# Attention: raw queries in the scores, the norm factor applied per token to the biased scores

## The chip, the cores and the metric

The kernel runs on one core of a Trainium2 chip. Five engines work side by side: TensorE (PE; its weight loads are listed as PEld), VectorE (DVE), ScalarE (ACT), GpSimd (POOL) and SyncE (SP, which only issues transfers here). The metric is the device time in microseconds; several runs are made, and their median is given.

## The reference

One step of a two-layer decoder over 1024 prompt tokens and 8 sample tokens, width 1024, all in fp32: layer 0 has a recurrent mixer, layer 1 sliding-window attention, and each is followed by a squared-ReLU MLP. The change lies in layer 1's attention: 16 query heads on 4 key/value heads of 64 columns, window 128, a linear distance bias per head, one learned sink per head, and an RMS norm of every query and key head.

```python
def rms_norm(x, g):
    xf = x.astype(jnp.float32)
    y = xf * lax.rsqrt(jnp.mean(xf * xf, axis=-1, keepdims=True) + RMS_EPS)
    return (y * g.astype(jnp.float32)).astype(x.dtype)

def qkv_heads(x, w_qkv, q_g, k_g):
    n, t, _ = x.shape
    q, k, v = jnp.split(x @ w_qkv, [Q_DIM, Q_DIM + KV_DIM], axis=-1)
    q = rms_norm(q.reshape(n, t, N_KV, GROUP, HEAD_DIM), q_g)
    k = rms_norm(k.reshape(n, t, N_KV, HEAD_DIM), k_g)
    return q, k, v.reshape(n, t, N_KV, HEAD_DIM)

def sink_attention(q, k, v, dist, mask, sinks):
    s = jnp.einsum('...qkgd,...skd->...kgqs', q, k).astype(jnp.float32) * (HEAD_DIM ** -0.5)
    s = s - alibi_slopes()[:, :, None, None] * dist.astype(jnp.float32)
    s = jnp.where(mask, s, NEG_INF)
    sink = sinks.astype(jnp.float32).reshape(N_KV, GROUP)[:, :, None, None]
    m = jnp.maximum(jnp.max(s, axis=-1, keepdims=True), sink)
    e = jnp.exp(s - m)
    p = e / (jnp.sum(e, axis=-1, keepdims=True) + jnp.exp(sink - m))
    return jnp.einsum('...kgqs,...skd->...qkgd', p.astype(v.dtype), v)
```

The outputs are the token stream, the new recurrent states, and the new keys (normed) and values.

## The kernel before

Tokens lie in the free dimension: a tile is 128 channels by 1032 tokens (T), worked in three chunks (c) of 344 (CH). To keep fp32 accuracy on fast passes, a value is split into a high part and a rest (hi, lo), and a product is three passes: hi·hi, hi·lo, lo·hi. A few small products are done in full fp32 instead; they show as two records each in the trace.

`attention` (L693) goes like this.

- **Projection.** Eight query tiles (t = 0 to 7, two heads each) and two key tiles (p = 0, 1). The first key and query tile are projected together (`proj_many`, L971), then the values (`v_proj`). The other eight units come from a generator, `filler` (L974): per tile `proj_steps` (L767) issues 24 groups of three matmuls into the three banks "P" (L772), one `yield` after each group.
- **Norm before.** `take_out` (L709) copies a finished bank twice on ScalarE (its square, L711, and itself, L712), after which the bank is free. `qk_norm` (L715) sums the squares over each head's 64 channels by a full fp32 matmul with a block matrix (L718, 344 columns, bank "N"), makes the factor in `rstd_m2` (L288: Ln, Exp, Square on ScalarE, L290 to L292; two VectorE operations, L293 and L295; it returns -2/rms) and multiplies (L720). `parts` splits the result (L730, L731), and SP sends its halves to their partitions (L747, L748; for keys L763). A unit has 24 + 1 + 3 = 28 yields.
- **Blocks.** 64 blocks (`STEPS`, L825), each 128 queries of one tile against up to 256 keys. `stage_a` (L840): four score matmuls (L852) into one of two banks "S"; on VectorE one custom operation per head (L856) that adds the bias from PSUM and SBUF, scales by -1 and finds the extreme against the sink; the exponential with its sum on ScalarE (L859); the reciprocal on VectorE (L861); the normalisation on GpSimd (L863). The bias is made on GpSimd once per tile, at its block 0 (`bias_of`, L834, L837). `stage_b`: four transposes (L872) and a copy (L877). `stage_c`, every fourth block: the products with the values (L893) and the split of the output (L900, L901).
- **Order.** The loop of L1013 runs `stage_a` three blocks ahead (`AHEAD`) and takes 3.9 yields of `filler` per block (`TF`) until block 46 (`J0`), where the rest is run out; from block 49 (`J1`) it takes 2.4 yields per block of the output projection (L1038). Under it a scheduler places each engine's instructions in one fixed order ahead of time; on the chip every engine works through its list in order and waits at semaphores.
- **Samples.** `samples` (L928) does the eight sample tokens during the output projection: 16 matmuls with the cached keys as weights (L933), softmax, 16 with the cached values (L958).

Of the kernel before, what the change touches and what calls it, by code (L numbers as in the profile page):

```python
# [60 lines left out]
def trunk(ctx: ExitStack, tc: tile.TileContext, I, O):  # L61
# [38 lines left out]
    def S(s="s"):  # L100
        return small["pool"].tile([P, CH], F32, tag="S", name=nm(s))
# [21 lines left out]
    def r_(x):  # L123
        return x.bitcast(F32R)
# [163 lines left out]
    def rstd_m2(ps, out=None):  # L288
        r0, q = S("r0"), S("q")
        act.activation(q, ps, AF.Ln, bias=eps)  # L290
        act.activation(r0, q, AF.Exp, scale=-0.5)
        last["rstd"] = act.activation(q, r0, AF.Square).ins  # L292
        dve.scalar_tensor_tensor(q, ps, eps, q, ALU.add, ALU.mult)  # L293
        out = r0 if out is None else out
        dve.scalar_tensor_tensor(out, q, -3.0, r0, ALU.add, ALU.mult)  # L295
        return out
# [396 lines left out]
    def attention(hs):  # L693
# [12 lines left out]
        ks = aux[:, P:P + 2 * NS].rearrange("p (t n) -> p t n", t=2)  # L706
        den = [cp.tile([P, 4], F32, name=f"den{i}") for i in range(4)]

# [6 lines left out]
        def qk_norm(sx, gcol):  # L715
            s, x = sx
            st = B("N")[:, :CH]
            pe.matmul(st, lhsT=blk, rhs=s, start=True, stop=True)  # L718
            r = rstd_m2(st)
            dve.scalar_tensor_tensor(x, x, gcol, r, ALU.mult, ALU.mult)  # L720
            return x
# [28 lines left out]
        def k_evac(p, c, sx):  # L750
            if c == 0:
                kst[p] = [(A("kh"), A("kl")) for _ in range(2)]
            k = qk_norm(sx, kg[:, 0:1])
            if c == 2:
                o = 2 * CH
                kout = S("kout")
                pool.tensor_copy(kout[:, :P], k[:, SEQ - P - o:SEQ - o])
                sp.dma_start(O["k"][p], kout[:, :P])
                pool.tensor_copy(ks[:, p, :], k[:, SEQ - o:T - o])
            for n, x in enumerate(parts(k)):  # L760
# [6 lines left out]
        def proj_steps(tag, w, evac):  # L767
# [59 lines left out]
        osm = aux[:, 2 * P:2 * P + 8 * NS].rearrange("p (t n) -> p t n", t=8)  # L827
# [6 lines left out]
        def bias_of(t):  # L834
            for u, hd in enumerate(heads(t)):
                o = (t % 2) * 512 + u * 256
                pool.tensor_scalar(bias2[:, o:o + 256], distM, -SLOPES[hd], 0.0, ALU.mult, ALU.add)  # L837


        def stage_a(j):  # L840
            t, b = STEPS[j]
            p, i = divmod(t, 4)
            if b == 0:
                bias_of(t)
# [9 lines left out]
            for u in range(2):  # L854
                o = (t % 2) * 512 + u * 256 + 256
                dve.tensor_tensor_reduce(  # L856
                    se[:, u, 256 - n:256], s[:, u * 256:u * 256 + n], bias2[:, o - n:o],
                    scale=-1.0, scalar=nsink[:, hd[u]:hd[u] + 1], op0=ALU.add, op1=ALU.min, accum_out=dn[:, u:u + 1])
# [69 lines left out]
        def samples():  # L928
            st = B("N")
# [6 lines left out]
            sb = S("ssb")  # L936
# [4 lines left out]
            dve.tensor_scalar(z[:, 129:257], z[:, 129:257], V("slope_row"), None, ALU.mult)  # L941
            dve.tensor_copy(z[:, 128:129], nsink_row)
            dd = cp.tile([P, 2], F32, name="dd")
            dve.tensor_tensor_reduce(z[:, 0:P], st2[:, :P], z[:, 129:257], scale=-1.0, scalar=nsink_row[:, 0:1],
# [26 lines left out]
        proj_many([wk, wq], hs, lambda i, c, o: (q_evac if i else k_evac)(0, c, take_out(o)))  # L971
        v_proj()

        def filler():  # L974
            for t in range(1, 8):
                if t == 4:
                    yield from proj_steps(("k", 1), unit("k", 1, 1), lambda *a: k_evac(1, *a))
                yield from proj_steps(("q", t), unit("q", t, 1 if t < 7 else 0), lambda *a, t=t: q_evac(t, *a))
# [401 lines left out]
```

## Time and profile before

| what | us |
|---|---|
| median of three runs (2017.08 to 2018.62) | 2017.08 |
| the profiled execution, in all | 2018.72 |
| its span, first to last instruction | 2016.9 |
| VectorE busy in it | 1411.6 |
| ScalarE busy in it | 1054.7 |
| GpSimd busy in it | 321.9 |

The span is what the profile's times add up to; the execution's own time has a little more around it. PE's busy time counts a matmul until its results are out, so overlapping matmuls make it look full: the pace is read from start to start. A group's row gives line, engine, operation, out<-in by the program's names, shape and count; then busy us, mean ns of one, and the idle time before it with what ended it. A row of waits reads: who, at which line, waited for whom: us in total, times, longest. A row of stretches: from:to, length, then busy us and count for PE, PEld, DVE, ACT, POOL; then the granted clock, the DMA engines' share and GB/s.

### The profile page before, as it was taken

Reading aid. Unit: us, or ns where it says so; the run is one execution under the profiler, and the core shown is the slowest. Engines: PE = TensorE matmul, PEld = TensorE weight load, DVE = VectorE, ACT = ScalarE, POOL = GpSimd, SP = SyncE. Lnnn points to the kernel's source line nnn. Section 1 sums busy time; section 2 is a strip of 40 time slices with the busy share of each in tenths; the row PEclk is TensorE's granted clock in tenths of the full one; section 3 lists DMA queues with packets and bytes.
Section 4 is the critical chain, followed back from the end, with each engine's and each line's share of the span. In section 5 each row is a group of like instructions: output and inputs, shape, how many; then the busy total and the mean of one; then the engine's idle time right before and its main releaser. Section 6 shows DMA issues by size and latency. Waiting matters only on the chain.

```text
span 2016.9 us, 38731 instructions
## 1 busy us (share of the span) xinstructions
PE 1995.5 (99%) x15106; PEld 1951.8 (97%) x15106; DVE 1411.6 (70%) x2665; ACT 1054.7 (52%) x2089; POOL 321.9 (16%) x570
## 2 busy tenths in 40 slices
PE   8999999999999999999999999999999999999999
PEld 8999999999999999999998887999999999999999
DVE  7996638877675876766847767579766667766662
ACT  6476536543434655554547776456443436555550
POOL 2420000000002233221004434000000003322220
PEclk9999999999999999999999999999999999999999
DMA  5111242343436788887333436612443447887783
GB/s 179 53 43 53 80 143 78 127 163 137 153 137 215 206 222 227 230 219 156 116 89 87 120 90 199 213 61 96 161 163 127 163 148 249 217 222 214 197 196 106
DMA packets 117927, 305.02 MB, mean 151 GB/s; under 512 B 17512, under 2 KB 50032, under 8 KB 117744
## 3 DMA queue, kind: packets, MB, share of 16 engines
q1 hardware_dynamic: 61744, 135.55, 22.0%
q0 software_dynamic: 28352, 98.30, 19.0%
q10 hardware_dynamic: 27648, 68.70, 9.3%
q8 instruction: 118, 1.93, 0.4%
q14 instruction: 65, 0.53, 0.1%
HBM read 176.30 MB, written 113.51 MB: 144 GB/s over the span
## 4 chain that ended last, share of the span: by engine, by line
PE 92%; DVE 4%; ACT 2%; issue 1%; DMA 1%; POOL 0%; SPq 0%; ACTq 0%; DVEq 0%
PE bD L530 60%; PE bP L227 12%; PE bS L227 6%; PE bP L772 4%; PE bT L227 3%; PE bS L852 1%; PE bO L893 1%; PE bT L872 1%; PE bN L718 1%; DVE sq L278 1%; PE bS L800 1%; DVE wl L167 0%; DMA raw<-w_in 0%; ACT wh L166 0%; DVE t L1189 0%
## 5 line engine op out<-in xcount | busy, mean ns | idle before, releaser
L530 PE MATMUL bD<-op,op 128*128 128x258 f32 x5376 | 648.0, 283 | 0.0
L530 PEld LDWEIGHTS bD<-op,op 128*128 128x128 f32 x5376 | 647.5, 190 | 0.3
L530 PE MATMUL bD<-tl,op 128*128 128x258 f32 x4704 | 567.7, 283 | 0.0
L530 PEld LDWEIGHTS bD<-tl,op 128*128 128x128 f32 x4704 | 566.7, 190 | 0.8 <-ACT he L637 0.3
L543 POOL DMA_DIRECT2D tl<-hsum x196 | 115.2, 698 | 899.1 <-DMA hsum<-he 405.2
L397 DVE TENSOR_TENSOR op<-ws,op 128x512 fp32r<-128x512 f32 (+2 forms) x288 | 170.3, 597 | 79.8 <-ACT op L396 79.8
L403 DVE TENSOR_TENSOR tl<-tl 128x516 fp32r<-128x516 f32 x196 | 130.8, 693 | 123.0 <-ACT tl L402 123.0
L637 ACT COPY ho<-bD 128x516 f32<-128x516 f32 x144 | 85.0, 590 | 243.8 <-PE bD L530 241.6
L396 ACT CAST op<-ws 128x512 fp32r<-128x512 f32 (+2 forms) x288 | 155.8, 550 | 56.0 <-DVE op L397 27.1
L397 DVE TENSOR_TENSOR op<-raw,op 128x512 fp32r<-128x512 f32 (+2 forms) x216 | 124.2, 595 | 57.7 <-ACT op L396 57.7
L637 ACT COPY he<-bD 128x516 f32<-128x516 f32 x144 | 84.0, 583 | 135.3 <-PE bD L530 127.0
L396 ACT CAST op<-raw 128x512 fp32r<-128x512 f32 (+2 forms) x216 | 114.6, 549 | 34.7 <-PE bD L530 22.5
L402 ACT CAST tl<-tl 128x516 fp32r<-128x516 f32 x196 | 114.8, 627 | 2.9 <-DMA tl<-hsum 2.9
L650 ACT ACTIVATE ho<-ho 128x1032 f32<-128x1032 f32 x32 | 34.2, 1069 | 107.2 <-DVE ho L649 107.2
L167 DVE TENSOR_TENSOR wl<-raw,wh 128x1024 fp32r<-128x1024 f32 (+1 forms) x57 | 66.0, 1164 | 23.5 <-ACT wh L166 13.2
L166 ACT CAST wh<-raw 128x1024 fp32r<-128x1024 f32 (+1 forms) x60 | 58.7, 988 | 38.8 <-DMA raw<-w_in 12.9
L863 POOL TENSOR_SCALAR se<-se,den 128x256 f32<-128x256 f32 (+1 forms) x128 | 65.7, 518 | 77.8 <-DVE den L861 75.8
L856 DVE CUSTOM_DVE_ANT_0 se<-bS,bias,nsink 128x256 f32<-128x256 f32 (+1 forms) x128 | 56.4, 461 | 21.2 <-PE bS L852 17.0
L859 ACT ACTIVATE se<-se,den 128x257 f32<-128x257 f32 (+1 forms) x128 | 63.0, 496 | 14.8 <-DVE den L856 13.1
L656 POOL DMA_DIRECT2D spill<-ho x32 | 28.5, 889 | 242.2 <-DVE ho L645 233.2
L645 DVE TENSOR_TENSOR ho<-bD,ho 128x516 f32<-128x516 f32 x72 | 49.7, 690 | 22.9 <-PE bD L530 22.9
L273 ACT ACTIVATE sq<-y 128x344 f32<-128x344 f32 x48 | 23.6, 492 | 71.4 <-DVE y L363 60.8
(300 smaller groups left out, 3727.3 us busy)
## 6 DMA issues: line engine op xcount, KB each, us to landing
tl<-hsum POOLq DMA_DIRECT2D x196, 258.0 KB, 7.8
raw<-w_up SPq DMA_DIRECT2D x64, 512.0 KB, 3.8
raw<-w_dn SPq DMA_DIRECT2D x64, 384.0 KB, 5.9
spill<-ho POOLq DMA_DIRECT2D x32, 516.0 KB, 6.6
spill<-he POOLq DMA_DIRECT2D x32, 516.0 KB, 7.9
hsum<-ho ACTq DMA_DIRECT2D x28, 516.0 KB, 3.6
hsum<-he ACTq DMA_DIRECT2D x28, 516.0 KB, 2.7
hsum<-ts ACTq DMA_DIRECT2D x28, 516.0 KB, 3.5
```

The source lines that it names most:

```text
L167: eng.tensor_tensor(r_(lo[:, sl]), raw[:, sl], hi[:, sl], ALU.subtract)
L227: pe.matmul(o, lhsT=r_(wt[:, col(k):col(k) + P]), rhs=r_(xt[:, cs(c)]), start=(k == first and a == 0), stop=(k == final and a == 2))
L396: act.copy(r_(t[:, 0:n]), src)
L397: dve.tensor_tensor(r_(t[:, n:2 * n]), src, t[:, 0:n], ALU.subtract)
L402: act.copy(r_(hi), lo)
L403: dve.tensor_tensor(r_(lo), lo, hi, ALU.subtract)
L530: pe.matmul(d[:, 512 * b:512 * b + QT], lhsT=r_(wt[:, j * P:j * P + P]), rhs=r_(xt[:, QT * b:QT * b + QT]), start=first and j == 0 and a = ...
L543: pool.dma_start(t[:, n:2 * n], src)
L637: last["copy"] = act.copy(t, f).ins
L772: pe.matmul(ps[c], lhsT=r_(wt[:, k * P:k * P + P]), rhs=r_(xt[:, cs(c)]), start=(k == 0 and a == 0), stop=(k == M8 - 1 and a == 2))
L859: act.activation(se[:, u, 256 - n:257], se[:, u, 256 - n:257], AF.Exp, scale=-1.0, bias=dn[:, u:u + 1], accum_out=dn[:, 2 + u:3 + u])
L863: pool.tensor_scalar(e, e, dn[:, 2 + u:3 + u], 0.0, ALU.mult, ALU.add)
```

## The change

Queries go raw (split, but not normed) into the scores. The key tile carries the keys' norm factor, both norm weights and a constant; the scores of a query token are then short of that token's own factor f. Since (s + d·slope/f)·f = s·f + d·slope, the bias is divided by f per token (GpSimd, per block, into a buffer that alternates by block), and the custom operation on VectorE multiplies by f instead of -1; f and 1/f are per-partition scalars there, because a block has its tokens on partitions. To have them so, the sums of squares are made with the squares as weights and two columns of the block matrix moving: eight matmuls of two columns per query tile, result 128 tokens by 16.

```diff
-    def rstd_m2(ps, out=None):
-        r0, q = S("r0"), S("q")
+    def rstd_m2(ps, out=None, n=CH):
+        r0, q = S("r0")[:, :n], S("q")[:, :n]
...
-        dve.tensor_scalar(qg, V("qg"), -0.0625, None, ALU.mult)
         dve.tensor_scalar(kg, V("kg"), -0.5, None, ALU.mult)
+        dve.tensor_scalar(qg, V("qg"), kg[:, 0:1], None, ALU.mult)
...
+        fac = aux[:, P + 2 * NS:P + 2 * NS + 16 * NS].rearrange("p (t k b u) -> p t k b u", t=4, k=2, u=2)
...
-        def q_evac(t, c, sx):
+        sqs = {}
+
+        def q_evac(t, c, o):
             p, i = divmod(t, 4)
             if c == 0:
                 qs[t] = (A("q0"), A("q1"))
-            q = qk_norm(sx, qg[:, 0:1])
+                sqs[t] = W("sq")
+            act.activation(sqs[t][:, cs(c)], o, AF.Square)
+            hi, lo = S("hi"), S("lo")
+            act.copy(r_(hi), o)
+            dve.tensor_tensor(r_(lo), o, hi, ALU.subtract)
             if c == 2:
-                o = 2 * CH
                 for u in range(2):
                     h = slice(64 * u, 64 * u + 64)
-                    pool.tensor_copy(qblk[h, :, p, u, i], q[h, SEQ - o:T - o])
-            hi, lo = parts(q)
+                    dve.tensor_copy(qblk[h, :, p, u, i], o[h, SEQ - 2 * CH:CH])
...
+        def q_factors(t):
+            s, st = sqs.pop(t), B("N")[:, :2 * NB]
+            for b in range(NB):
+                pe.matmul(st[:, 2 * b:2 * b + 2], lhsT=s[:, b * P:b * P + P], rhs=con[:, C_BLK:C_BLK + P:64], start=True, stop=True)
+            r = S("r")[:, :2 * NB]
+            rstd_m2(st, r, 2 * NB)
+            f = fac[:, t % 4]
+            dve.tensor_scalar(f[:, 0], r.rearrange("p (b u) -> p b u", u=2), 0.0625, None, ALU.mult)
+            dve.reciprocal(f[:, 1], f[:, 0])
...
-            k = qk_norm(sx, kg[:, 0:1])
+            x, r = k_norm(take_out(o))
             if c == 2:
                 o = 2 * CH
-                kout = S("kout")
-                pool.tensor_copy(kout[:, :P], k[:, SEQ - P - o:SEQ - o])
+                kout = S("kout")[:, :P + NS]
+                dve.scalar_tensor_tensor(kout, x[:, SEQ - P - o:T - o], kg[:, 0:1], r[:, SEQ - P - o:T - o], ALU.mult, ALU.mult)
...
+            dve.scalar_tensor_tensor(x, x, qg[:, 0:1], r, ALU.mult, ALU.mult)
+            for n, x in enumerate(parts(x)):
...
-            sx = [take_out(o) for o in ps]
-            yield
-            for c in range(NCH):
-                evac(c, sx[c])
+            yield from evac(ps)
+            done.add(tag)
+
+        def q_out(t):
+            def f(ps):
+                for c in range(NCH):
+                    q_evac(t, c, ps[c])
                 yield
-            done.add(tag)
+                yield
+                q_factors(t)
+                yield
+            return f
...
             for u in range(2):
-                o = (t % 2) * 512 + u * 256 + 256
+                o = (j % 2) * 512 + u * 256 + 256
+                pool.tensor_scalar(bias2[:, o - n:o], distM[:, 256 - n:256], fac[:, t % 4, 1, b, u:u + 1], SLOPES[hd[u]],
+                                   ALU.mult, ALU.mult)
+            for u in range(2):
+                o = (j % 2) * 512 + u * 256 + 256
                 dve.tensor_tensor_reduce(
                     se[:, u, 256 - n:256], s[:, u * 256:u * 256 + n], bias2[:, o - n:o],
-                    scale=-1.0, scalar=nsink[:, hd[u]:hd[u] + 1], op0=ALU.add, op1=ALU.min, accum_out=dn[:, u:u + 1])
+                    scale=fac[:, t % 4, 0, b, u:u + 1], scalar=nsink[:, hd[u]:hd[u] + 1], op0=ALU.add, op1=ALU.min, accum_out=dn[:, u:u + 1])
...
         def samples():
+            sb = S("ssb")
+            act.activation(sb[:, :P], qrow, AF.Square, scale=4.0)
+            st = B("N")
+            pe.matmul(st[:, 0:1], lhsT=sb[:, :P], rhs=ones[:, 0:1], start=True, stop=True)
+            r = S("r")[:, :1]
+            rstd_m2(st[:, 0:1], r, 1)
+            dve.tensor_scalar(dd[:, 2:3], r, 0.0625, None, ALU.mult)
...
+            dve.tensor_scalar(qrow, qrow, V("qg"), None, ALU.mult)
+            yield
```

A key tile is evacuated the same way (`k_out`: three chunks, a yield after each), so every unit now has 24 + 3 = 27 yields; `AHEAD`, `TF` and the rest of the loop's numbers stay. The sample queries are held raw and get their factor in `samples`, as a row's scalar, in the same way.

The scheduler's order moves with it. On TensorE, right behind the last matmul of query tile 1's projection, before (bP: projection, bS: scores, bN: sums of squares):

```order
L772 MATMUL bP_11959<-hh_10798,wl_11717 128x344
L852 MATMUL bS_12034<-kh_11437,q_11491 128x256
L852 MATMUL bS_12034<-kl_11438,q_11491 128x256
L852 MATMUL bS_12034<-kh_11439,q_11492 128x256
L852 MATMUL bS_12034<-kl_11440,q_11492 128x256
L718 MATMUL bN_12062<-sq_12048,con 128x344
L772 MATMUL bP_12121<-hh_10784,wh_11953 128x344
L772 MATMUL bP_12121<-hl_10785,wh_11953 128x344
```

and now:

```order
L787 MATMUL bP_11943<-hh_10798,wl_11682 128x344
L872 MATMUL bS_12016<-kh_11433,q_11487 128x256
L872 MATMUL bS_12016<-kl_11434,q_11487 128x256
L872 MATMUL bS_12016<-kh_11435,q_11488 128x256
L872 MATMUL bS_12016<-kl_11436,q_11488 128x256
L757 MATMUL bN_12064<-con,sq_12034 128x2 x5
L787 MATMUL bP_12089<-hh_10784,wh_11937 128x344
L787 MATMUL bP_12089<-hl_10785,wh_11937 128x344
L787 MATMUL bP_12089<-hh_10784,wl_11938 128x344
L757 MATMUL bN_12064<-con,sq_12034 128x2 x3
```

Where one sum of squares over 344 tokens stood, and two more some way on, a tile's eight small ones now stand in two bursts (16 bursts for the eight tiles).

On GpSimd, around the tenth to fifteenth block, before (se: a block's scores, den: its reciprocal, bias: the bias, aux: sample queries):

```order
L863 TENSOR_SCALAR se_11384<-se_11384,den_11377 128x256 x2
L847 COPY se_11385<-nsink 128x2
L744 COPY aux<-x_12286 64x8 x2
L863 TENSOR_SCALAR se_11385<-se_11385,den_11378 128x256 x2
L847 COPY se_11384<-nsink 128x2
L863 TENSOR_SCALAR se_11385<-se_11385,den_11379 128x256 x2
```

and now (aux holds the factors):

```order
L876 TENSOR_SCALAR bias_11383<-con,aux 128x256 x2
L887 TENSOR_SCALAR se_11385<-se_11385,den_11378 128x256
L867 COPY se_11385<-nsink 128x2
L887 TENSOR_SCALAR se_11385<-se_11385,den_11378 128x256
L876 TENSOR_SCALAR bias_11383<-con,aux 128x256 x2
L887 TENSOR_SCALAR se_11385<-se_11385,den_11379 128x256 x2
```

The two biases of a coming block stand between the normalisations of the earlier ones.

On TensorE, right behind the last matmul of the last projection (query tile 7), before:

```order
L772 MATMUL bP_13999<-hh_10798,wl_13660 128x344
L872 MATMUL bT_14220<-con,se_11385 128x128 x4
L718 MATMUL bN_14228<-sq_14208,con 128x344
L852 MATMUL bS_14262<-kh_12963,q_13602 128x256
L852 MATMUL bS_14262<-kl_12964,q_13602 128x256
L852 MATMUL bS_14262<-kh_12965,q_13603 128x256
L852 MATMUL bS_14262<-kl_12966,q_13603 128x256
```

and now:

```order
L787 MATMUL bP_13941<-hh_10798,wl_13620 128x344
L872 MATMUL bS_14162<-kh_12877,q_13235 128x256
L872 MATMUL bS_14162<-kl_12878,q_13235 128x256
L872 MATMUL bS_14162<-kh_12879,q_13236 128x256
L872 MATMUL bS_14162<-kl_12880,q_13236 128x256
L896 MATMUL bT_14210<-con,se_11385 128x128 x4
L757 MATMUL bN_14216<-con,sq_14180 128x2 x5
```

From that last matmul to where the output projection's matmuls (L227) run on, there were four score blocks and are now seven.

More of the change, by code (lines that the diff above doesn't have):

```diff
@@ L774, in proj_steps, with k_out, f @@
                     yield
-            sx = [take_out(o) for o in ps]
-            yield
-            for c in range(NCH):
-                evac(c, sx[c])
-                yield
-            done.add(tag)
+            yield from evac(ps)
[4 more added lines that the diff above has]
+                    q_evac(t, c, ps[c])
+                yield
+                yield
+                q_factors(t)
+                yield
+            return f
+        def k_out(p):
+            def f(ps):
+                for c in range(NCH):
+                    k_evac(p, c, ps[c])
+                    yield
+            return f
         v_tiles = [W("vt") for _ in range(2)]
@@ L928, in samples @@
         def samples():
+            sb = S("ssb")
[5 more added lines that the diff above has]
+            dve.tensor_scalar(dd[:, 2:3], r, 0.0625, None, ALU.mult)
+            dve.reciprocal(dd[:, 3:4], dd[:, 2:3])
+            dve.tensor_tensor(dd[:, 3:4], dd[:, 3:4], V("slope_row"), ALU.mult)
+            dve.tensor_scalar(qrow, qrow, V("qg"), None, ALU.mult)
+            yield
             st = B("N")
@@ L935, in samples @@
                     yield
-            sb = S("ssb")
             dve.tensor_copy(sb[:, :P], st[:, :P])
@@ L976, in filler @@
                 if t == 4:
[L977 to L978 removed]
+                    yield from proj_steps(("k", 1), unit("k", 1, 1), k_out(1))
+                yield from proj_steps(("q", t), unit("q", t, 1 if t < 7 else 0), q_out(t))
         def load_o(t, sl):
```

28 lines of the change are left out of this document (10 added, 18 removed).

## The prediction

> **What bounds the kernel now.** I read the page first, then the stretches of the attention stage, then the groups of TensorE's matmuls, its waits and single rows of its timeline. The page says that TensorE is the bound:
>
> ```profile
> span 2016.9 us, 38731 instructions
> PE 1995.5 (99%) x15106; PEld 1951.8 (97%) x15106; DVE 1411.6 (70%) x2665; ACT 1054.7 (52%) x2089; POOL 321.9 (16%) x570
> PE 92%; DVE 4%; ACT 2%; issue 1%; DMA 1%; POOL 0%; SPq 0%; ACTq 0%; DVEq 0%
> ```
>
> The chain that ends last is 92% TensorE. So an instruction taken from VectorE, ScalarE or GpSimd gains only what TensorE waits for it. The change lies between about 1011 us (key and query projection) and 1276 us (last attention block), and at 1300 us for the eight sample tokens. The table of stretches there (busy time of PE, weight loads, VectorE, ScalarE, GpSimd, each with its count):
>
> ```profile
> 1045.00:1148.00 103.00, 102.40 (x687) 90.33 (x684) 69.33 (x241) 71.42 (x211) 37.15 (x92) 1.00 0.38 100
> 1148.00:1218.00 70.00, 66.18 (x443) 57.67 (x440) 48.59 (x168) 50.38 (x148) 27.68 (x67) 1.00 0.36 96
> 1218.00:1233.00 15.00, 13.35 (x86) 8.71 (x85) 11.24 (x36) 12.79 (x35) 6.63 (x17) 1.00 0.23 64
> 1233.00:1276.00 43.00, 41.66 (x275) 32.37 (x274) 32.45 (x119) 27.83 (x84) 17.21 (x43) 1.00 0.87 279
> ```
>
> Until 1218 us projection matmuls fill the pauses of the attention blocks. In the 15 us from 1218 the projections have run out, and the output projection has not yet set in: weight loads are busy 8.71 of 15 us. That is the one thin place. The clock is granted in full (1.00), so nothing is to be had there. What waits:
>
> ```profile
> PE bP L772 <- ACT x L712: 2.0, 1, 2.0
> PEld bP L772 <- ACT x L712: 2.5, 2, 2.3
> PEld bT L872 <- POOL se L847: 4.6, 6, 1.1
> PEld bT L872 <- POOL se L863: 4.4, 12, 0.4
> L872 PE MATMUL bT<-con,se 128*128 128x128 f32 x240 | 38.5, 277 | 3.1 <-ACT pt L877 2.0 <-DVE pt L877 0.9
> ```
>
> The transposes (L872) already wait for GpSimd's normalisation, 4.6 and 4.4 us in 18 places, at the weight load; of this the array itself shows less (3.1 us idle before L872 in all). There was one wait of 2.0 us for free projection banks.
>
> **TensorE's own work: what goes.** 24 of the 30 sums of squares over 344 tokens go (eight query tiles of three chunks); the six of the keys stay.
>
> ```profile
> L718 PE MATMUL bN<-sq,con 128*128 128x344 f32 x60 | 24.0, 482 | 0.7 <-ACT sq L711 0.6
> 1110.82 0.48 PE L772 MATMUL bP<-hl,wh 128*128 128x344 f32 x2
> 1111.15 0.74 PE L718 MATMUL bN<-sq,con 128*128 128x344 f32 x2
> 1111.46 0.58 PE L772 MATMUL bP<-hl,wh 128*128 128x344 f32 x1
> 1111.88 0.28 PE L852 MATMUL bS<-kh,q 128*128 128x256 f32 x1
> ```
>
> Each is full fp32 and shows as two records: 60 records, 24.0 us busy, so 0.80 us each at most, with fill and waits. In a quiet place it is 1111.15 to 1111.88, less the 0.16 us of the L772 in between: 0.57 us. I take the middle, 0.69: 24 x 0.69 = 16.5 us go (13.7 to 19.2).
>
> **What comes.** 64 matmuls, eight per query tile, with the squares as weights (128x128, fp32) and two columns moving. The nearest row is L958 of the samples: fp32, weights 128x128, eight columns moving, seven of them on end.
>
> ```profile
> 1317.59 0.32 PE L227 MATMUL bS<-oh,wh 128*128 128x344 f32 x1
> 1317.89 1.73 PE L958 MATMUL bN<-ssb,vc 128*128 128x8 f32 x14
> 1319.48 0.40 PE L227 MATMUL bS<-ol,wh 128*128 128x344 f32 x1
> ```
>
> From 1317.89 to 1319.48 are 1.59 us for seven, 0.227 us each: what a matmul with so few columns costs is its two weight loads, not its columns. 64 x 0.227 = 14.5 us. Going in costs up to 0.14 us more (1317.59 to 1317.89 against 0.16); the program issues them in 16 bursts, so up to 2.3 us; I take half: 15.6 us (14.5 to 16.8). So on TensorE the two forms are nearly even: -16.5 + 15.6 = **-0.9 us**. The samples get one more such matmul and its entry, and seven of their sixteen now come in one burst: **+0.5 us** (0 to 1).
>
> The Trainium skill (TensorE: Matmul & The Clock Gate, section Back-to-back issue gap) gives a sustained spacing of about 81 ns for a pair of weight load and matmul at 128 columns moving; as an estimate from that page, 128 passes would be 10.4 us, and the change 4 us better than my sum. The trace does not agree: L958's passes lie 1.59 us / 14 = 114 ns apart, and this row is of the same type and weight size, so the measurement decides.
>
> **ScalarE and VectorE: less work, little of it on the path.** Per query chunk Ln, Exp and Square of the factor go from ScalarE, and three 344-wide operations from VectorE:
>
> ```profile
> L290 ACT ACTIVATE q<-bN,vec 128x344 f32<-128x344 f32 x30 | 16.7, 556 | 3.3 <-PE bN L718 3.0 <-DMA od0h<-o 0.2
> L292 ACT ACTIVATE q<-r 128x344 f32<-128x344 f32 x30 | 14.7, 491 | 0.5
> L291 ACT ACTIVATE r<-q 128x344 f32<-128x344 f32 x30 | 14.7, 490 | 0.5
> L293 DVE SCALAR_TENSOR_TENSOR q<-bN,vec,q 128x344 f32<-128x344 f32 x30 | 17.2, 574 | 19.3 <-ACT q L292 19.3
> L295 DVE SCALAR_TENSOR_TENSOR r<-q,r 128x344 f32<-128x344 f32 x30 | 15.5, 518 | 0.4
> L720 DVE SCALAR_TENSOR_TENSOR x<-x,qg,r 128x344 f32<-128x344 f32 x24 | 14.0, 582 | 0.4
> L861 DVE RECIPROCAL den<-den 128x1 f32<-128x1 f32 x128 | 19.5, 157 | 21.0 <-ACT se L859 20.6
> ```
>
> 24 x (0.556 + 0.491 + 0.490) = 36.9 us go from ScalarE, 24 x (0.574 + 0.518 + 0.582) = 40.2 us from VectorE. Back come, per tile, three and four operations on 16 columns, some 0.2 us each (L861, one column, 0.16): 8 x 7 x 0.2 = 11 us over both. The keys get two more VectorE operations of 136 columns and lose two GpSimd copies. TensorE's matmuls cover all of this, so I cost it at nothing; were the cover gone, it would be those 11 us. There is one exception. The projection banks used to be free after two ScalarE operations; now a VectorE subtraction that reads the bank stands behind them, and behind whatever VectorE has queued. That subtraction is new on the bank's release and costs about 0.5 us (the 344-wide rows above), while the relief of both engines shortens their queues. If the 2.0 us wait of L772 goes, -2.0; if each of seven later tile changes shows the subtraction, 7 x 0.5 = +3.5. I take **-1 us**, since two engines with 37 and 40 us less to do are more often ready.
>
> A query tile's first block also gets ready sooner, which I cost at nothing as well. The two halves used to leave for SBUF behind the norm; now they leave right behind the copy and the subtraction, with the same 96 transfers on SP:
>
> ```profile
> q<-hi SPq DMA_DIRECT2D x48, 86.0 KB, 2.1
> ```
>
> What is late now is the factor: eight small matmuls (1.8 us), three operations on ScalarE and four on VectorE (1.4), the bias (0.5), 3.7 us together, beside the transfer's 2.1 and not behind it.
>
> **GpSimd: more work, in front of the scores.** The bias was made once per tile, 16 times; now it is made for every block, 128 times, since it is divided by the token's factor, and the score operation on VectorE waits for it.
>
> ```profile
> L863 POOL TENSOR_SCALAR se<-se,den 128x256 f32<-128x256 f32 x112 | 58.6, 528 | 39.5 <-DVE den L861 37.8
> L847 POOL COPY se<-nsink 128x2 f32<-128x2 f32 x64 | 16.0, 252 | 50.8 <-PE bT L872 49.0 <-PE bT L800 1.5
> L837 POOL TENSOR_SCALAR bias<-con 128x256 f32<-128x256 f32 x12 | 5.2, 433 | 3.4 <-DVE den L856 2.8
> ```
>
> 128 at 0.43 to 0.53 us are 55 to 68 us, less the 16 old ones (6.9 us): GpSimd gets about 55 us more. A block then has 2 x 0.48 + 2 x 0.528 + 0.252 = 2.3 us on GpSimd, while 13 score blocks (52 rows of L852 below) take 43 us, 3.3 us each: not the bound, but near. GpSimd works in order: a bias behind a normalisation that waits for its reciprocal holds up the next score operation on VectorE, then its exponential, and the two score banks. The transposes' 9.0 us of waiting for GpSimd rests on 37 + 28 + 7 + 17 = 89 us of work from 1045 us on; with 55 more I expect it to grow by about six tenths, 5 us at the weight loads, of which the array shows a part: **+2 us** (-1, if GpSimd's queue is slack everywhere and VectorE's relief helps, to +9, the whole wait doubled).
>
> The Trainium skill (SBUF — State Buffer, section Who interferes with whom) says that a VectorE instruction with two SBUF inputs and a GpSimd instruction that reads SBUF exclude each other. By it the change would relieve GpSimd: the queries' operations with two SBUF inputs go, and the new subtraction reads one from PSUM. No run here separates this; it is a reason for the lower end of the range.
>
> **The blocks that lose their filler.** A projection tile now has 27 places where other work may be put between, not 28; eight units give eight fewer, at 3.9 per block two blocks. So the projections run out two blocks earlier; in the scheduler's order seven score blocks stand between their last matmul and the output projection's run, where four stood, one of the three having only been placed later than it was. Their price comes from the 15 us stretch:
>
> ```profile
> 1218.00:1233.00 15.00, 3.00 (x16) 2.23 (x16) 1.00 0.23 64
> 1233.00:1276.00 43.00, 8.94 (x52) 7.38 (x52) 1.00 0.87 279
> ```
>
> (L852 alone, four rows a block.) Four blocks there, and 15 - 8.71 = 6.3 us without a weight load, 1.6 us each: three more cost up to 4.7 us. But in that stretch ScalarE was busy 12.79 of 15 us, much of it with the last tile's norm, which is now short; so the lower end is 0, and I take a third, **+1.5 us**.
>
> **Sum.** -0.9 + 0.5 - 1 + 2 + 1.5 = +2.1 us on a span of 2016.9, so 2019.0 us. The profiled execution took 2018.72 us in all, 1.8 more than its span; the median of the three runs shown is 2017.08, so the runs lie near the span and I put the sum on the median: 2019.2, said as **2019 us**. A measurement of this kernel can tell about 0.2%, 4 us, from no change: 2013 to 2021.
>
> **Rivals.**
> Faster: the relief counts. The quiet matmul price is too low for what goes (0.80: 19.2 us), bursts enter free (14.5), the waits of L772 (2.0) and those of L872 for the copies (3.1) go, the bare stretch shrinks: -19.2 + 14.5 - 5.1 + 0.5 = -9.3, so 2008. For it speaks that ScalarE and VectorE stand at 12.79 and 11.24 of 15 us where TensorE idles; against it that TensorE idles only 7.4 us from 1045 to 1276 by the table (0.6 + 3.8 + 1.7 + 1.3). 0.22.
>
> Slower: GpSimd in front of the scores. In the blocks from 1218 on (17) and at the seven tile changes, where three blocks come on end, the bias waits behind a normalisation and the score operation behind the bias; 0.5 us for each of 17 + 21 blocks is 19 us at the engines, half of it on TensorE: +9.5, with the sum's other terms 2026. It decides once a block's 2.3 us on GpSimd, with its wait for the reciprocal, exceed the 3.3 us per block. For it: 18 of the 64 blocks wait for GpSimd even now; against: blocks are issued three ahead. 0.26.
>
> Also slower: the banks. All seven tile changes stall for the subtraction with VectorE's queue before it, 0.5 + 0.5 us each: +7, 2024. 0.10.
>
> Moved, not gained: 0.42 for the forecast, whose own range is 2014 to 2023. Faster than 0.2% is the first rival and a sliver of the forecast, 0.23; slower is 0.26 + 0.10 and a little, 0.37; the rest, 0.40, is the same. With the rivals' ends the range is 2010 to 2028.
>
> **What would show it.** The sum on TensorE: the new two-column matmuls at 0.22 to 0.25 us from start to start, against 0.57 or more for the keys' remaining six. GpSimd: bias rows of 0.43 to 0.53 us, and L872's waits for GpSimd between 10 and 18 us. The bare blocks: seven score blocks between the last projection and the output projection's run, with some 8 us without a weight load. Wrong would be: GpSimd named as what VectorE's score operation waits for, by tens of us, or waits for GpSimd that vanish.

## The result and the profile after

| | before | after |
|---|---|---|
| median, us (six runs each, one chip) | 2018.14 (2017.08 to 2021.52) | 2009.47 (2007.03 to 2011.25) |
| ratio, 95% interval | | 0.9954 [0.9941, 0.9967] |
| profiled execution, its span | 2018.72, 2016.9 | 2008.62, 2006.8 |

The change makes the kernel 0.46% faster, some 9 us. The forecast said 2019; the time lies just under the lower end of its range, close to where the first rival had put it (2008). The page of the changed kernel, the lines that answer to those of before:

```profile
span 2006.8 us, 38904 instructions
PE 1990.0 (99%) x15188; PEld 1957.9 (98%) x15188; DVE 1393.3 (69%) x2649; ACT 1018.1 (51%) x2021; POOL 363.6 (18%) x664
PE 95%; DVE 2%; ACT 1%; DMA 1%; issue 1%; POOL 0%; SPq 0%; DVEq 0%; ACTq 0%
```

TensorE issues 82 records more and yet ends 10.1 us earlier. VectorE is busy 18 us less, ScalarE 37 us less, GpSimd 42 us more. Two things in this the prediction did not count. From ScalarE four operations per query chunk go, not three: the copy of the bank (L712) goes too, since the high part is now taken straight from the bank. And VectorE's score operation became dearer. The rows before (the score operation now is L880, below):

```profile
L712 ACT COPY x<-bP 128x344 f32<-128x344 f32 x27 | 12.3, 457 | 2.2 <-DMA kl<-x 1.3 <-DMA kh<-hi 1.0
L856 DVE CUSTOM_DVE_ANT_0 se<-bS,bias,nsink 128x256 f32<-128x256 f32 (+1 forms) x128 | 56.4, 461 | 21.2 <-PE bS L852 17.0
```

It takes 461 ns in the kernel before and 522 now, 7.8 us in all. With the bias made per tile again in the changed kernel (a run below) it still takes 521, and with the bias per block in the kernel before 461. So the longer time goes with the factor as its scale in place of -1, not with GpSimd's bias. The stretches, cut at the same places of the program as before (columns as there):

```profile
1043.00:1146.00 103.00, 102.14 (x719) 94.49 (x719) 63.37 (x234) 59.49 (x189) 57.21 (x138) 0.98 0.38 102
1146.00:1210.00 64.00, 63.12 (x457) 57.72 (x454) 41.55 (x162) 35.69 (x120) 38.68 (x96) 1.00 0.36 96
1210.00:1225.00 15.00, 13.88 (x101) 10.20 (x101) 11.63 (x47) 11.63 (x37) 9.83 (x24) 1.00 0.61 164
1225.00:1265.00 40.00, 37.83 (x270) 31.71 (x269) 30.29 (x106) 24.18 (x72) 28.42 (x64) 1.00 0.77 261
```

The second stretch has shrunk from 70 to 64 us, the last from 43 to 40. Seven score blocks stand between the last projection and the output projection's run, as expected, but the bare 15 us are no thinner than before: 10.20 us of weight loads where 8.71 stood. The groups of TensorE and GpSimd in the stage, and all waits of the transposes' weight loads for GpSimd:

```profile
L757 PE MATMUL bN<-con,sq 128*128 128x2 f32 x128 | 15.9, 245 | 1.0 <-ACT sq L742 0.9
L876 POOL TENSOR_SCALAR bias<-con,aux 128x256 f32<-128x256 f32 (+1 forms) x128 | 63.5, 497 | 62.2 <-DVE den L880 30.7 <-DVE aux L762 20.9 <-DVE aux L761 3.0
L880 DVE CUSTOM_DVE_ANT_0 se<-bS,bias,nsink 128x256 f32<-128x256 f32 (+1 forms) x128 | 64.2, 522 | 22.6 <-PE bS L872 18.8 <-POOL bias L876 1.4 <-POOL se L867 1.1
```

```profile
PEld bT L896 <- POOL se L887: 3.8, 10, 0.4
PEld bT L896 <- POOL se L867: 1.3, 2, 1.0
PEld bT L896 <- POOL bias L876: 1.2, 3, 0.4
```

GpSimd's new bias rows take 0.497 us, inside the predicted 0.43 to 0.53, but little waits for them: VectorE's score operation 1.4 us in all, the transposes 3.8 + 1.3 + 1.2 = 6.3 us for GpSimd, less than the 9.0 of before. The waits for free projection banks (2.0 and 2.5 us) have no successor.

Idle columns hide short waits, since PE counts as busy until results are out. The next table therefore takes all of TensorE's starts from the first sum of squares to the last product with the values, and compares the time between them with the quiet pace of each kind (0.158 us for a 344-column pass, 0.118 for 256 columns of scores or of the value projection, 0.288 for a pass of a norm matmul, 0.112 for a two-column pass; the transposes and the products with the values, 57.7 us together, at one pace in both kernels). What exceeds the pace is waiting, slow clock included:

| part of the stage | before: us (waiting) | after: us (waiting) |
|---|---|---|
| to the end of the value projection | 35.1 (1.9) | 32.3 (0.2) |
| query and key tiles to the fifth | 97.1 (3.7) | 95.4 (3.2) |
| to the end of the projections | 73.6 (6.6) | 71.5 (2.2) |
| to the last product with the values | 57.3 (9.5) | 55.2 (6.9) |
| sum | 263.1 (21.7) | 254.4 (12.4) |

TensorE's own work is as good as unchanged (241.4 and 242.0 us); what shrank is its waiting, by 9 us, in all four parts. The level of 21.7 us hangs on the paces taken; the difference hardly does, since the same paces stand on both sides.

### The profile page after: what moved, and what is told of

It reads as the page before. It is cut to its first block, busy times and chain, and to the rows that moved or that the text cites. A ratio compares the mean times of both kernels' runs of the same rounds, so it can differ in the third digit from the quotient of the medians.

```text
span 2006.8 us, 38904 instructions
## 1 busy us (share of the span) xinstructions
PE 1990.0 (99%) x15188; PEld 1957.9 (98%) x15188; DVE 1393.3 (69%) x2649; ACT 1018.1 (51%) x2021; POOL 363.6 (18%) x664
## 3 DMA queue, kind: packets, MB, share of 16 engines
q0 software_dynamic: 28352, 98.30, 19.2%
## 4 chain that ended last, share of the span: by engine, by line
PE 95%; DVE 2%; ACT 1%; DMA 1%; issue 1%; POOL 0%; SPq 0%; DVEq 0%; ACTq 0%
PE bD L530 61%; PE bP L227 13%; PE bS L227 7%; PE bP L787 4%; PE bT L227 4%; PE bO L917 1%; PE bT L896 1%; PE bS L872 1%; PE bS L828 1%; PE bN L757 1%; DMA raw<-w_in 0%; DVE se L880 0%; DVE sq L278 0%; DMA raw<-w_out 0%; DVE wl L167 0%
## 5 line engine op out<-in xcount | busy, mean ns | idle before, releaser
L397 DVE TENSOR_TENSOR op<-raw,op 128x512 fp32r<-128x512 f32 (+2 forms) x216 | 124.5, 597 | 57.4 <-ACT op L396 57.3
L880 DVE CUSTOM_DVE_ANT_0 se<-bS,bias,nsink 128x256 f32<-128x256 f32 (+1 forms) x128 | 64.2, 522 | 22.6 <-PE bS L872 18.8
L876 POOL TENSOR_SCALAR bias<-con,aux 128x256 f32<-128x256 f32 (+1 forms) x128 | 63.5, 497 | 62.2 <-DVE den L880 30.7
L887 POOL TENSOR_SCALAR se<-se,den 128x256 f32<-128x256 f32 (+1 forms) x128 | 61.4, 486 | 8.5 <-DVE den L885 6.2
```

The source lines that it names most:

```text
L397: dve.tensor_tensor(r_(t[:, n:2 * n]), src, t[:, 0:n], ALU.subtract)
L876: pool.tensor_scalar(bias2[:, o - n:o], distM[:, 256 - n:256], fac[:, t % 4, 1, b, u:u + 1], SLOPES[hd[u]], ALU.mult, ALU.mult)
L880: dve.tensor_tensor_reduce(se[:, u, 256 - n:256], s[:, u * 256:u * 256 + n], bias2[:, o - n:o], scale=fac[:, t % 4, 0, b, u:u + 1], scalar ...
```

## The experiments

Each kernel ran with the kernel before on one chip; ratios are to that. One thing had to be kept apart. Each execution records its mean granted clock, and within a kernel the time follows it. The run with narrow VectorE operations (below) shows it best, twelve executions of one program:

| mean granted clock | 1.000 | 0.999 | 0.998 | 0.995 | 0.994 | 0.993 | 0.992 |
|---|---|---|---|---|---|---|---|
| us (mean, executions) | 2008.5 (1) | 2010.1 (2) | 2011.7 (3) | 2015.6 (1) | 2017.9 (3) | 2019.5 (1) | 2020.9 (1) |

A fit with one slope for all kernels gives 1.46 us per 0.001. So beside each median stands the mean of its executions set to clock 1.000 with that slope ("at 1.000"); there the kernel before is 2017.6 (2017.2 to 2017.9 on the four chips of the runs below) and the changed one 2007.2, 10.4 us apart. Differences of about 1 us mean nothing. The setting takes out a slower clock also where the edit itself brings it about, so the medians stand beside it.

A second thing could not be kept apart. The scheduler places the whole program anew for each edit. In the two runs that touch only GpSimd's bias TensorE's order stays practically as it was; in the others it moves. So each price below is that of some operations together with the order that comes with them.

**The load put back.** To the changed kernel's query chunk, ScalarE's three and VectorE's three norm operations are added again, on scratch that nobody reads (the bank's copy is not); then each engine's alone.

```diff
+            ja = S("ja")
+            act.activation(ja, sqs[t][:, cs(c)], AF.Ln, bias=eps)
+            act.activation(ja, ja, AF.Exp, scale=-0.5)
+            act.activation(ja, ja, AF.Square)
+            jd, sq = S("jd"), sqs[t][:, cs(c)]
+            dve.scalar_tensor_tensor(jd, sq, eps, sq, ALU.add, ALU.mult)
+            dve.scalar_tensor_tensor(jd, jd, -3.0, sq, ALU.add, ALU.mult)
+            dve.scalar_tensor_tensor(jd, jd, qg[:, 0:1], sq, ALU.mult, ALU.mult)
```

> The changed kernel, with the load that it took from ScalarE and VectorE put back: per query chunk three 344-wide operations on each of the two, on scratch, which nobody waits for. If the gain came from shorter queues on these two (relief): 5 to 7 us slower than the changed kernel, about 2015. If it came from the exchange of matmuls on TensorE, or from the order: at most 1 us slower, about 2010.

> The changed kernel, with only ScalarE's three 344-wide operations per query chunk put back on scratch. If ScalarE's queue alone carries the relief: about 9 us slower than the changed kernel, 2019. If both share it: some 3 to 6 us. If it is VectorE's: within 1 us.

> The changed kernel, with only VectorE's three 344-wide operations per query chunk put back on scratch. If VectorE's queue alone carries the relief: about 9 us slower than the changed kernel. If both share it: some 3 to 6 us. If it is ScalarE's: within 1 us.

Measured: both 2019.13 us, 0.9995 [0.9986, 1.0003]; ScalarE's alone 2012.64, 0.9967 [0.9955, 0.998]; VectorE's alone 2021.84, 1.0011 [1.0001, 1.0021]. At 1.000 they are 2013.6, 2009.4 and 2012.9, so 6.4, 2.2 and 5.7 us over the changed kernel, and the clock takes the rest. With the load back, the gain in the median is gone, and VectorE's share is the larger. The timeline with VectorE's load shows how it costs (start, duration, engine, line, and in brackets the idle time before):

```profile
1223.91 0.28 PE L876 MATMUL bS<-kl,q 128*128 128x256 f32 x1
...
1223.92 0.52 DVE L745 TENSOR_TENSOR lo<-bP,hi 128x344 fp32r<-128x344 f32 x1 [0.54 <-ACT hi L744]
...
1224.36 0.57 DVE L749 SCALAR_TENSOR_TENSOR jd<-jd,qg,sq 128x344 f32<-128x344 f32 x1
1224.84 0.57 DVE L747 SCALAR_TENSOR_TENSOR jd<-sq,vec 128x344 f32<-128x344 f32 x1
...
1225.45 0.52 DVE L748 SCALAR_TENSOR_TENSOR jd<-jd,sq 128x344 f32<-128x344 f32 x1
...
1226.20 0.58 DVE L749 SCALAR_TENSOR_TENSOR jd<-jd,qg,sq 128x344 f32<-128x344 f32 x1
...
1226.96 0.53 DVE L884 CUSTOM_DVE_ANT_0 se<-bS,bias,nsink 128x256 f32<-128x256 f32 x1
...
1228.11 0.58 PE L876 MATMUL bS<-kh,q 128*128 128x256 f32 x1 [3.92 <-DVE den L884]
```

The scores are ready at 1224.2, but VectorE works through its list in order, and the norm work put back (L747 to L749, with the split L745) stands in front of the score operation L884, which starts at 1226.96. TensorE stands still for 3.92 us until a score bank comes free. VectorE as a whole is far from full (71% of the span); here the score operation's place in line is what costs.

**The same operations, 16 columns wide.**

```diff
+            jd, sq = S("jd")[:, :16], sqs[t][:, c * CH:c * CH + 16]
```

> The changed kernel with the same three VectorE operations per query chunk as in the run that put VectorE's load back, in the same places and with the same inputs, but 16 columns wide instead of 344. The full width cost 11 to 13 us over the changed kernel. If VectorE's busy time is what costs, these 72 short operations (about 6 us of VectorE instead of some 40) cost under 3 us over the changed kernel: 2008 to 2012 us beside a kernel before at 2017 to 2019. If it is the instructions themselves, their place in the queue or their waits for ScalarE's squares, the loss stays: 2018 to 2022 us.

2013.7 us, 0.9974 [0.9961, 0.9987]; at 1.000 it is 2008.9, 1.7 over the changed kernel, against 5.7 at full width. At equal clock it is mainly the time in the queue that costs, not the number of instructions. The median misses the 2008 to 2012 that the load theory gave, because this run had the clock from 1.000 to 0.992.

**The kernel before, relieved step by step.** First without VectorE's three norm operations of the queries, then without ScalarE's three too, then without the norm matmuls too.

```diff
             st = B("N")[:, :CH]
             pe.matmul(st, lhsT=blk, rhs=s, start=True, stop=True)
+            if gcol is qcol:
+                r0, q = S("r0"), S("q")
+                act.activation(q, st, AF.Ln, bias=eps)
+                act.activation(r0, q, AF.Exp, scale=-0.5)
+                act.activation(q, r0, AF.Square)
+                return x
...
+        qcol = qg[:, 0:1]
...
-            q = qk_norm(sx, qg[:, 0:1])
+            q = qk_norm(sx, qcol)
```

(In the second the three activations are left out; in the third the `return` stands ahead of the matmul.)

> The kernel before without the three VectorE operations that norm the queries (the queries enter the scores un-normed and unscaled, so the output leaves the norm out); TensorE's norm matmuls and ScalarE's logarithm, exponential and square stay. If VectorE's relief is most of what the change brought, this alone takes 6 to 9 us off the kernel before, 2009 to 2012 us. If the gain needs the changed order, the later release of the banks or ScalarE's relief, it takes 0 to 3 us off, 2015 to 2018 us.

> The kernel before with the queries' three VectorE norm operations and ScalarE's logarithm, exponential and square left out (the queries enter the scores un-normed; the norm matmuls stay, unread). Without VectorE's three alone it took 2011.7 us, 7 less than the kernel before. If ScalarE's relief is worth the 2 to 3 us that putting the same load back into the changed kernel cost, this takes 2008.5 to 2010 us. If ScalarE's relief counts only where the banks are released in the changed order, it stays at 2011 to 2012.5 us.

> The same, and the queries' 24 norm matmuls left out too. If they count one for one in the relieved kernel before, at 0.66 to 0.70 us each as where they were added to the changed kernel, 16 to 17 us go: 1992 to 1994 us, and the changed kernel's 64 two-column matmuls and factors then cost 15 to 17 us over this. If part of them lies in waits that come back, as with the small ones (two thirds), 10 to 11 us go: 1998 to 2000 us, and the small ones cost some 10.

| kernel | median, us | ratio to before | at 1.000 | step |
|---|---|---|---|---|
| before | 2019.12, 2019.41 | | 2017.6 | |
| no VectorE norm | 2011.66 | 0.996 [0.9947, 0.9973] | 2011.5 | -6.1 |
| no ScalarE norm either | 2006.84 | 0.9942 [0.993, 0.9955] | 2006.9 | -4.6 |
| no norm matmuls either | 1998.15 | 0.9893 [0.9878, 0.9908] | 1995.7 | -11.2 |
| the changed kernel | 2009.47 | 0.9954 [0.9941, 0.9967] | 2007.2 | +11.5 |

The first two steps make up 10.7 us, as much as the whole change brings; the last two, TensorE's exchange with all that goes with the new form (factors, biases, the dearer score operation, one ScalarE copy less, the order), cancel to +0.3. ScalarE's step is larger than either theory expected (2 to 3, or nothing). TensorE's waiting, counted as in the table above, falls with the steps: some 22 us before, 17 without VectorE's three operations, 10 without ScalarE's too. It rises again to 14 when the norm matmuls go, which fits that these bring 11.2 us and not the 13.8 of their pace (24 x 2 x 0.288). What the steps leave open is the order: without VectorE's three operations the scheduler already places seven score blocks between the last projection and the output projection's run, as in the changed kernel, where the kernel before has four. A run with less load in the old order was not made. In the stretches with the chain out, the projections' second half is 66 us, as against 70, with TensorE busy through it, and the blocks behind the bare stretch are 37 as against 43:

```profile
1145.00:1211.00 66.00, 65.95 (x452) 57.76 (x451) 37.21 (x144) 38.27 (x122) 24.19 (x67) 1.00 0.38 101
1211.00:1226.00 15.00, 14.07 (x86) 8.62 (x85) 10.89 (x43) 12.19 (x38) 6.95 (x21) 1.00 0.45 116
1226.00:1263.00 37.00, 36.88 (x270) 31.71 (x268) 28.24 (x102) 23.68 (x71) 15.56 (x39) 1.00 0.91 303
```

**TensorE's prices.** 24 unread norm matmuls are added to the changed kernel; and its eight small matmuls per tile are replaced by one.

```diff
+            pe.matmul(B("N")[:, :CH], lhsT=blk, rhs=sqs[t][:, cs(c)], start=True, stop=True)
```

```diff
-            for b in range(NB):
-                pe.matmul(st[:, 2 * b:2 * b + 2], lhsT=s[:, b * P:b * P + P], rhs=con[:, C_BLK:C_BLK + P:64], start=True, stop=True)
+            pe.matmul(st, lhsT=s[:, 0:P], rhs=con[:, C_BLK:C_BLK + 2 * NB], start=True, stop=True)
```

> The changed kernel, with the 24 full fp32 sums of squares of 344 columns put back beside the new small matmuls; nobody reads them. TensorE's work counts one for one: 24 x 0.57 = 13.7 us to 24 x 0.80 = 19 us slower than the changed kernel. If they fill pauses: less than 10 us.

> The changed kernel with one 16-column matmul per query tile in place of the eight two-column ones (it leaves out the sums of squares of seven of the eight token blocks, so the factors of those tokens are not theirs). If TensorE's work counts one for one here, 56 matmuls at 0.224 us start to start go: 12.5 us faster than the changed kernel, some 1996 to 1998 us. If TensorE waits for the other engines anyway, the gain shows up again as waiting: under 4 us, 2005 us or more.

Added: 2026.17 us, 1.0038 [1.0025, 1.0052]; at 1.000 +15.9 over the changed kernel, 0.66 us per norm matmul. Left out: 2000.73, 0.9909 [0.9895, 0.9922]; at 1.000 -7.9 for 56 matmuls, 0.14 us each, where 0.224 is their pace. That lies between the two expectations. What TensorE gains on a leaner list partly turns into waiting (12.4 us of it in the changed kernel, 18.2 in this run; 1.8 of it is a projection matmul that waits for the subtraction which frees its bank).

**GpSimd's bias and the places for other work.** The bias per block on GpSimd alone, in the kernel before; the bias once per tile again in the changed kernel (not divided by the factors); one `yield` per unit less in the kernel before (27 places); one more in the changed kernel (28).

```diff
             for u in range(2):
-                o = (t % 2) * 512 + u * 256 + 256
+                o = (j % 2) * 512 + u * 256 + 256
+                pool.tensor_scalar(bias2[:, o - n:o], distM[:, 256 - n:256], -SLOPES[hd[u]], 0.0, ALU.mult, ALU.add)
...
```

(The run also drops `bias_of` and its call at a tile's block 0.)

```diff
+            if b == 0:
+                for u in range(2):
+                    o = (t % 2) * 512 + u * 256
+                    pool.tensor_scalar(bias2[:, o:o + 256], distM, -SLOPES[hd[u]], 0.0, ALU.mult, ALU.add)
             for u in range(2):
-                o = (j % 2) * 512 + u * 256 + 256
-                pool.tensor_scalar(bias2[:, o - n:o], distM[:, 256 - n:256], fac[:, t % 4, 1, b, u:u + 1], SLOPES[hd[u]],
-                                   ALU.mult, ALU.mult)
```

```diff
             sx = [take_out(o) for o in ps]
-            yield
```

```diff
                 yield
                 yield
+                yield
                 q_factors(t)
...
             def f(ps):
+                yield
                 for c in range(NCH):
                     k_evac(p, c, ps[c])
```

> The kernel before, with the bias made on GpSimd for every block instead of once per tile (112 more GpSimd operations, nothing else). The prediction's GpSimd term: +2 us, up to +9, against the kernel before. If GpSimd's queue is slack: within 1 us.

> The changed kernel, with the bias made once per tile and not divided by the token's factor (the output's bias is then scaled wrongly; 112 GpSimd operations fewer). The prediction's GpSimd term: 2 us faster than the changed kernel, up to 9. If GpSimd's queue is slack: within 1 us of it.

> The kernel before, with 27 places per projection unit instead of 28 (one yield left out), so that the projections run out two blocks earlier as in the change. The prediction's bare blocks: +1.5 us, up to +4.7. If the finer order is what gained: 2 to 6 us faster than before.

> The changed kernel with 28 places per projection unit again (one yield more), so that the projections last two blocks longer. If the 4.8 us that the 27 places cost the kernel before are lost in the changed kernel too: 3 to 5 us faster than the changed kernel, about 2005. If the relief has already covered the bare blocks: within 1 us.

| edit | median, us | ratio to before | at 1.000 |
|---|---|---|---|
| before, bias per block | 2019.12 | 1.0003 [0.9994, 1.0012] | +1.1 on before |
| after, bias per tile | 2010.15 | 0.9957 [0.9944, 0.9969] | -0.6 on after |
| before, 27 places | 2023.11 | 1.0024 [1.0015, 1.0033] | +3.0 on before |
| after, 28 places | 2008.24 | 0.9948 [0.9935, 0.996] | +0.3 on after |

112 more operations on GpSimd cost about a microsecond at most, in either kernel. A place fewer costs 3 us in the kernel before and nothing in the changed one. That bare blocks have a price where VectorE's list holds the norm work is the reading that fits; no run tries it by itself. The kernel with 28 places is not to be told from the changed one.

**More relief for VectorE.** Every second of VectorE's copies of transposed weights goes to ScalarE.

```diff
-            (act.copy if t % 2 else dve.tensor_copy)(dst, src)
+            (act.copy if j % 4 else dve.tensor_copy)(dst, src)
```

> The changed kernel with every second of VectorE's copies of transposed weights given to ScalarE: 32 copies of about 0.65 us leave VectorE by half, some 10 us less there, some 9 us more on ScalarE. By what the loads put back cost (11 to 13 us for some 40 us of VectorE, 2 to 3 us for some 44 us of ScalarE, if both go on evenly below the load of the changed kernel): 2.5 to 3 us gained and 0.5 us lost, 2006 to 2007 us. If VectorE's load only costs above a threshold that the changed kernel is already under, nothing is gained: 2008.5 to 2011 us.

2012.86 us, 0.9971 [0.996, 0.9982]; at 1.000 it is 2010.5, 3.3 over the changed kernel. The run got slower, which neither theory had. The copies did move:

```profile
L901 ACT COPY pt<-bT 128x512 f32<-128x512 f32 (+1 forms) x48 | 27.0, 562 | 16.3 <-PE bT L896 16.0
L901 DVE COPY pt<-bT 128x512 f32<-128x512 f32 (+1 forms) x16 | 9.8, 615 | 2.8 <-PE bT L896 2.7
```

11 us off VectorE gained nothing, and with 9 us more on ScalarE the kernel lost 3.3 us, where 38 us of norm work put back on ScalarE had cost 2.2. That the copies hold up the exponentials on ScalarE is a guess; the order moved too. A price per microsecond of load does not carry over from one kind of work to another.

## Why the prediction was wrong

- **The relief of ScalarE and VectorE, costed at nothing but -1 for the banks, was the step that failed**: "TensorE's matmuls cover all of this, so I cost it at nothing". Taken out of the kernel before, VectorE's three operations give 6.1 us and ScalarE's three 4.6, each with the order that the scheduler then makes. The banks' release was part of it (the 2.0 us wait is gone), not all. The list of what goes was short as well: it left out ScalarE's copy (24 x 0.457 = 11 us) and the dearer score operation on VectorE (+7.8 us). Neither has a run of its own.
- **Its ground was a wrong reading.** Against the rival I held that TensorE idles only 7.4 us in the stage. That is what the idle column shows, which starts to count only when the last result is out; from start to start, 21.7 us were waiting (19.8 without the value projection), and only 11 of the distances between starts are longer than half a microsecond. The weight loads' waits gave a hint: all their rows in this stage add up to some 31 us before and 20 after, and the prediction read three of them (2.5, 4.6 and 4.4 us).
- **The first rival's time was right, its sum only in part, so its 2008 is partly luck.** It named the relief, the bank waits and the bare stretch, but had 4.7 of its 9.3 us from TensorE's exchange (-19.2 + 14.5), which brought nothing.
- **TensorE's exchange, -0.9:** nearly even, as said. The two-column matmuls run at 0.224 us from start to start (0.22 to 0.25 was predicted), an added norm matmul costs 0.66 at equal clock and 0.70 by the medians (0.69 was taken). In place, with the waits that come and go and with all else of the new form, the two sides are -11.2 and +11.5.
- **GpSimd, +2 and the rival at 2026:** about 0. The transposes' waits for it fell to 6.3 us where 10 to 18 was forecast, though its bias rows rose as computed. A wait for GpSimd is at bottom one for the exponential and the reciprocal ahead of it, and those now come sooner; that reading is argued from the rows, not tried by itself.
- **Bare blocks, +1.5:** about 0 in the changed kernel (28 places: +0.3), 3.0 in the kernel before. The term fits the loaded kernel; that the change took its ground away together with the load is argued, as above. The expected 8 us without a weight load in the stretch were 4.8.
- **The banks, 2024:** did not come; no wait of a projection matmul for its banks is left.
- **What stays open:** how the 10.7 us divide among single waits, and how much of them is the load and how much the order. Putting the same operations back in the changed kernel, at another place in the queues, gives 6.4 of them back at equal clock.

## What to carry to other kernels

Where TensorE is "99% busy", sum its start-to-start distances against the quiet pace of each kind before calling another engine's work covered: here 19.8 us of waiting lay under an idle column of 7.4 for the same stretch. An in-order engine at 70% can still stand in the way; ask what lies ahead of the operation that frees the next bank, not how full the engine is. And terms of one change can act on each other: the price of bare blocks, 3.0 us in the loaded kernel, was about 0 in the changed one.

## What the runs showed of the hardware

TensorE's granted clock drops to half for some microseconds; in the traces each drop that ends inside the execution lasts 3.4 us or two or three times that. In the profiled execution with narrow VectorE operations four such drops, 27 us at half the clock, cost 14 us of full clock, and it took 11 us more than the execution at clock 1.000. That such drops make the spread of the other kernels too is argued from the mean clocks. The stretches of 4 us around two of them, in the kernel with VectorE's load put back (the last three numbers are granted clock, DMA share and GB/s):

```profile
1052.00:1056.00 4.00, 3.91 (x31) 3.83 (x29) 1.62 (x6) 2.45 (x6) 0.68 (x2) 1.00 0.09 22
1056.00:1060.00 4.00, 4.00 (x18) 4.00 (x18) 4.00 (x10) 2.15 (x9) 3.08 (x5) 0.57 0.70 138
...
1224.00:1228.00 4.00, 0.19 (x2) 0.00 (x0) 3.90 (x14) 0.90 (x4) 0.00 (x0) 0.91 0.55 128
1228.00:1232.00 4.00, 3.54 (x13) 2.65 (x13) 3.26 (x20) 2.85 (x13) 2.84 (x7) 0.50 0.92 276
1232.00:1236.00 4.00, 4.00 (x24) 3.24 (x25) 2.89 (x8) 2.83 (x8) 3.56 (x8) 0.74 0.93 299
```

The second follows the pause of 3.92 us: 0.91 up to 1228, 0.50 from there. The Trainium skill (TensorE: Matmul & The Clock Gate, section Part 1: The HAM clock gate (the "warmup" mystery)) states that an idle window of about 3.4 us halves the clock and that the window runs freely; this pause agrees. A window that runs freely could also be why executions of one program differ, which no run here separates. But shorter pauses were followed by 0.50 as well: pauses of 2.25 and 0.77 us with one group of transposes between them in the kernel with narrow operations, and a single one of 1.41 us in the kernel before without VectorE's norm operations. And the first drop follows no pause. The changed kernel has it too:

```profile
1054.30 1.44 PE L757 MATMUL bN<-con,sq 128*128 128x2 f32 x10
1055.60 0.40 PE L787 MATMUL bP<-hh,wh 128*128 128x344 f32 x1
...
1056.16 0.72 PE L757 MATMUL bN<-con,sq 128*128 128x2 f32 x6
1056.74 0.41 PE L787 MATMUL bP<-hh,wh 128*128 128x344 f32 x1
```

```profile
1056.00:1060.00 4.00, 4.00 (x23) 4.00 (x22) 2.99 (x11) 2.20 (x9) 1.76 (x7) 0.71 0.48 112
1060.00:1064.00 4.00, 4.00 (x26) 4.00 (x25) 1.08 (x6) 0.88 (x4) 1.36 (x4) 0.87 0.60 138
```

Sixteen two-column passes within 2.5 us, with three projection passes among them, stand right before it, with TensorE "busy" all along, and the clock is 0.71 and 0.87 in the next two stretches: 0.29 x 4 + 0.13 x 4 = 1.7 us lost. In the kernels with 28 places and with the added norm matmuls a drop follows such a burst too (at 1168.8 and 1153.3 us). It looks as if passes with two columns count as idle for the clock; no run separates that, and in this profile seven of the eight tiles show no drop.
